# Second and last FFN of a two-layer decoder: third weight chunk without its displaced head, and no one-column product ahead of it

## The chip, the cores and the metric

The kernel runs on one core of one Trainium2 chip. The metric is the device time of one execution in microseconds (us); the median of three runs stands for a kernel.

## The reference

A causal decoder trunk of two layers on 256 tokens of width 1024, all in float32. Each layer adds half an FFN, a mixer and half an FFN again; every FFN is a SwiGLU of width 2816:

```python
def swiglu(x, w_gate, w_up, w_down):
    return (jax.nn.silu(x @ w_gate) * (x @ w_up)) @ w_down

for layer in range(DEPTH):                                   # 2
    h = h + 0.5 * swiglu(rms_norm(h, ffn1_norm[layer]), ...)
    h = h + (ab_mixer if layer == 0 else c_mixer)(rms_norm(h, mix_norm[layer]))
    h = h + 0.5 * swiglu(rms_norm(h, ffn2_norm[layer]), ...)
return rms_norm(h, final_norm)
```

So there are four FFNs. The second (phase 2 in the kernel) is the one behind the first layer's mixer, the last (phase 5) the one behind the second layer's; the third (phase 3) follows the second at once.

## The kernel before

**Products.** Each float32 operand is split into a high part, rounded to the type fp32r, and a low part, the remainder. One product of two matrices is three on TensorE (`mm3`, lines 389 to 391): high by high, low by high, high by low. Activations lie transposed in SBUF, `xTh` and `xTl`, eight tiles k of 128 rows by 256 tokens. In the gate and up parts of an FFN a weight tile of 128x128 is what TensorE holds (loaded by the record PEld) and 256 columns of `xTh` or `xTl` stream past it.

**The weight stream.** `weight_chunks` lists all weights as chunks of 2048 columns per partition, in the order of use; a gate or up chunk is 8 tiles k of 256 columns. `Stream` loads each by DMA from SP's queue into one of three `raw` tiles (line 202), then splits it into one of four pairs `whi`, `wlo`: high part by ScalarE (ACT, line 250), low part by VectorE (DVE, line 257). A chunk without a head is split in two pieces of 1024 columns. `st.take()` hands a chunk to TensorE, `st.free()` gives it back.

**The order in an FFN.** Chunk n alternates gate and up. For chunk n the loop in `ffn` takes a chunk and makes 48 products of 256 columns into one PSUM bank (`colwise`): 24 with the chunk's first 128 columns, then 24 with the other half; the first chunk alone goes by parts of k (`TURNS`), since its input is still being made. After chunk 2 (`late` is 3) two products form the sums for the norm (lines 482, 483), and SiLU and the products with up follow on DVE and ACT (`gated`). After 22 chunks come the down projections; the last FFN does these with products of 512 columns in `finish`.

**Addresses.** A chunk's columns begin 16 elements into their tile (`SHIFT`), and buffers, `xTh` and `xTl` are laid out so that in the gate, up and down products of 256 columns the next weight tile and the running stream stand 16 elements apart, modulo 64. A chunk with `reset=3` (`RESET`, given in `weight_chunks` for the chunk numbers in `again`) has the first 128 columns of its tiles k = 0, 1, 2 elsewhere:

```python
h = w // 2
far = nk * w - reset * h + RESHIFT // LINE * LINE + RESHIFT     # 2048 - 384 + 0 + 52
def part(t, k):
    if k >= reset:
        return t[:, at(k) : at(k) + w]
    return Halves(*(t[:, a : a + h] for a in (far + k * h, shift + k * h)))
```

1664 is a multiple of 64, so these three tiles stand 52 elements from the stream, modulo 64, where all others stand 16. They are used by the first nine products of the chunk (3 tiles by 3 products): this is the head. Such a chunk is split in three pieces, 384, 384 and 1280 columns. Heads stand in all four FFNs and in both mixers; in the first and third FFN many stand behind groups of other products that are woven in (`seven_products`).

**The product of one column.** In phases 2 and 5, behind the second chunk (n = 1), `ffn` multiplies a tile of ones by one column of ones into a bank that nobody reads (line 817). It is plain float32, and the records show it as two matmuls. The chunk behind it, n = 2, is the one with the head.

**What orders the engines.** A scheduling layer writes each engine's program from the code; instructions on one engine run in that order, and engines wait for each other by semaphores. In the last FFN DVE also transposes x (`turn_back`, line 713) and SP stores the result (`away`).

Of the kernel before, what the change touches and what calls it, by code (L numbers as in the profile page):

```python
# [54 lines left out]
def weight_chunks():  # L55

    chunks = []

    def add(m, r, n, c0, c1, shift=0, cuts=(), reset=0, summed=False, kind="N"):
        chunks.append((m[:-1], m[-1], r, n, c0, c1, shift, cuts, reset, summed, kind))  # L60

    def cols(m, c0, w, cuts=(), reset=0):
        n = CH // w
        for k in range(0, KD, n):
            add(m, k * 128, n, c0, c0 + w, SHIFT if w == 256 else 0, cuts, reset)

    def ffn(name, layer, last=False, again=(2, 3), phase=None):
        first = len(chunks)
        wd = (f"{name}_w_down", layer)
        lag = LAGS.get(phase, FT)  # L70
        woven = phase in LAGS

        def seven(pair):
            add(wd, pair * 256, 2, 0, 512, MSHIFT, kind="S")

        for c in range(0, FF, 256):
            if len(chunks) == 0:
                for k in (0, 4):
                    add((f"{name}_w_gate", f"{name}_w_up", layer), k * 128, 4, c, c + 256, SHIFT,
                        (1, 2, 3) if k else (0.5, 1, 1.5, 2, 3))  # L80
                continue
            for m in ("gate", "up"):
                n = len(chunks)
                cuts = (6,) if first == 0 and n in again else ()
                cols((f"{name}_w_{m}", layer), c, 256, cuts,
                     RESET if n - first in again or woven and m == "gate" and c // 256 > lag else 0)
            if c // 256 >= lag:
                seven(c // 256 - lag)
        if last:
            for i in range(FT // 2):  # L90
                add(wd, i * 256, 2, 0, D, kind=LAST[i])
            return
        rest = list(range(FT // 2 - lag, FT // 2)) if woven else []
        behind = woven
        if lag > 2 and woven:
            seven(rest.pop(0))
        for c in range(512 if woven else 0, D, 256):
            for k, n in DOWN:
                add(wd, k * 128, n, c, c + 256, SHIFT, reset=RESET if behind or woven and (c, k) == (768, 16) else 0)
                behind = bool(rest)  # L100
                if rest:
                    seven(rest.pop(0))

    def mix(m, order, summed=False):
        for k in order[:4:2]:
            add(m, k * 128, 2, 0, D, SHIFT)
        for c in (0, 512):
            add(m, order[4] * 128, 4, c, c + 512, SHIFT, summed=summed and c == 0)

    ffn("ffn1", 0, again=(2,), phase=0)  # L110
    wab = ("ab_w_in", 0)
    cols(wab, 0, 256)
    cols(wab, 512, 256, reset=RESET)
    cols(wab, 1024, 512)
    cols(wab, 2048, 512)
    for c, n in ((1536, RESET), (1792, 0), (256, RESET), (768, RESET)):
        cols(wab, c, 256, reset=n)
    mix(("ab_w_out", 0), MIX1)
    ffn("ffn2", 0, again=(2,), phase=2)
    ffn("ffn1", 1, again=(), phase=3)  # L120
    wc = ("c_w_in", 0)
    for c in range(4):
        cols(wc, c * 256, 256, reset=RESET if c % 2 else 0)
        cols(wc, 1024 + c * 256, 256, reset=0 if c else RESET)
        if c % 2 == 0:
            cols(wc, 2048 + c * 256, 512)
    mix(("c_w_out", 0), MIX2, True)
    ffn("ffn2", 1, True, again=(2,))
    return chunks


# [215 lines left out]
def trunk(ctx: ExitStack, tc: tile.TileContext, a, out):  # L347
    nc = tc.nc
# [10 lines left out]
    def bank():  # L359
        return ps.tile([128, 512], F32, name="bank")  # L360

    st = Stream(tc, (raw_pool, hi_pool, lo_pool), a["weights"])
    for ms, _, _, n, c0, c1, *how in weight_chunks():
        st.add(n, len(ms) * (c1 - c0), *how)
# [8 lines left out]
    ones = cp.tile([128, 128], F32, name="ones")  # L373
# [19 lines left out]
    def split(hi, lo, src):  # L393
        return nc.scalar.activation(hi, src, AF.Copy), nc.vector.tensor_sub(lo, src, hi.bitcast(F32))  # L394
# [131 lines left out]
    def colwise(p, w, groups=((0, range(KD)), (1, range(KD)))):  # L526

        n = 0
        for j, ks in groups:
            cs = slice(j * 128, (j + 1) * 128)  # L530
            for k in ks:
                mm3(p[:, j * S : (j + 1) * S], w[0][k][:, cs], w[1][k][:, cs], xT["h"][:, k], xT["l"][:, k],
                    n == 0, n == 2 * KD - 1)
                n += 1
# [154 lines left out]
    def ffn(phase):  # L689
        nonlocal nxt  # L690
        with tc.tile_pool(name="fp", bufs=1) as fp:
# [16 lines left out]
            def turn_back(t):  # L708

                with tc.issue_after(nxt.low.ins):  # L710
                    turned = xn.rearrange("p (j k r) -> p j k r", j=4, k=KD)
                    for k in range(KD):
                        nc.vector.transpose(turned[:, :, k],
                                            x1(k)[:, t * 128 : (t + 1) * 128].rearrange("p (j c) -> p j c", j=4))
                    nc.sync.dma_start(away[t], xn)
# [35 lines left out]
            def seven_products(c):  # L751

                if not sevens:
                    sevens.extend(bank() for _ in range(4))
                w = st.take()
                plain = [[h[:, 2 * c + k, t * 128 : (t + 1) * 128] for h in hT] for k, t in ((0, 0), (1, 0), (1, 1))]
                s3, s1, s2, s4 = ([h[:, i] for h in summed[c]] for i in range(4))
                a11, a12, a22 = plain
                for i, (at, (sh, sl), q) in enumerate(((0, a11, 0), (1, a12, 2), (2, s4, 1), (3, a22, 6), (4, s1, 3),
                                                       (5, s2, 5), (6, s3, 4))):  # L760
                    b = sevens[at // 2][:, at % 2 * S : (at % 2 + 1) * S]
                    mm3(b, sh, sl, w[0][q], w[1][q], c == 0 and at % 2 == 0, c == FT // 2 - 1 and at in (1, 3, 5, 6))
                st.free()
                summed.pop(c)
# [27 lines left out]
            def sums_at(n):  # L792

                if (phase, n) in AHEAD:
                    ahead.append(begin_sums(fp, AHEAD.index((phase, n))))
                if (phase, n - 1) in AHEAD:
                    ahead.append(ahead.pop()())
                if (phase, n - 2) in AHEAD:
                    ahead.pop()()
# [4 lines left out]
            for n in range(FT):  # L804
                k, m = n - n % 2, n % 2
                if phase == n == 0:
                    with tc.manual_schedule():
                        ready += begin(fp)
                elif phase or n > 1:
                    p = bank()  # L810
                    w = st.take()
                    colwise(p, w, *(() if n else (TURNS,)))
                    st.free()
                    ready.append(p)
                if phase in (2, 5) and n == 1:

                    nc.tensor.matmul(bank()[:, :1], ones, ones[:, :1], start=True, stop=True)
                sums_at(n)
                if n == late - 1:
                    if phase not in (2, 5):  # L820
                        split(*parts[:2], nxt.acc[:, 0])
                    nxt.everywhere(*parts)
                    if last:
                        half = nxt.column(norm["half"], parts[3][:, :128], "halfcol")
                if last and n in (6, 9):
                    turn_back(n // 9)
                    flat = X.rearrange("p i c -> p (i c)")
                    if n == 9:
                        st.spare.append(flat[:, :CH])
                if last and n == late:  # L830
                    hS = [fp.tile(size, F32R, name=m) for m in ("hSh", "hSl")]
                if n == late:
                    for i in range(0, n, 2):
                        gated(i, *ready[i : i + 2])
                elif n > late and m == 1:
                    gated(k, *ready[-2:])
                if m == 1 and k // 2 >= lag:
                    seven_products(k // 2 - lag)
# [546 lines left out]


    ffn(0)
    ab_mixer(1)
    ffn(2)
    ffn(3)  # L1390
    c_mixer(4)
    ffn(5)
# [19 lines left out]
def _layout(a):  # L1412

    def tiles(m):
        return m.reshape(-1, 128, m.shape[-1]).transpose(1, 0, 2)

    chunks = weight_chunks()
    weights = np.zeros((len(chunks), 128 * CH), np.float32)
    for j, (ms, layer, r, n, c0, c1, *how) in enumerate(chunks):
# [43 lines left out]
```

## Time and profile before

| | before |
|---|---|
| median of 3 runs | 920.46 us (920.32 to 920.67) |
| the profiled execution's own time | 919.95 us |
| its span | 918.2 us |
| TensorE (PE) busy | 910.9 us, 99%, 7533 matmuls |
| DVE busy, ACT busy | 774.4 us (84%), 562.4 us (61%) |
| chain that ended last | PE 99% |
| granted TensorE clock | 0.999 of full |
| the one-column products (line 817) | from 283.08 and from 748.44 us |

Times in the views are us from the span's start. A row of the timeline is start, length, engine, line, operation, output <- inputs, shape, and the count of merged records. A matmul's record lasts longer than the step to the next one, since matmuls overlap: a product of 256 columns has a record of 0.28 us and starts 0.11 us behind the one before. So PE is "busy" throughout, and what tells its speed is the step from start to start, or a count of products over a stretch. The clock does not appear in a row of the timeline; the view of stretches has it.

### The profile page before, as it was taken

The numbers are of one execution on the slowest core, as the hardware profiler recorded it, in microseconds if no ns is written. First come the engines' busy times: TensorE is split into PE (matmuls) and PEld (weight loads), VectorE is DVE, ScalarE is ACT, GpSimd is POOL, SyncE is SP. The second block draws the span as 40 slices with busy tenths as digits, with TensorE's granted clock in tenths as the row PEclk, the third lists the DMA queues.
The fourth block names the chain that finished last, engine by engine and source line by source line (L and its number), as shares of the span: only waits on it lengthen the run. The fifth ranks groups of instructions, "written<-read, shape, count | busy, mean of one in ns | idle before, by whom it ended". The sixth has DMA issues, their size and how long they took to land.

```text
span 918.2 us, 18470 instructions
## 1 busy us (share of the span) xinstructions
PE 910.9 (99%) x7533; PEld 892.0 (97%) x7533; DVE 774.4 (84%) x1269; ACT 562.4 (61%) x875; POOL 81.3 (9%) x117
## 2 busy tenths in 40 slices
PE   9999999999999999999999999999999999999997
PEld 9999999989999999999999999999999999999886
DVE  7999897997889777767799888878778799978897
ACT  7766555668667545444566555556777776555574
POOL 0000000034310000000000000001665100000001
PEclk9999999999999999999999999999999999999999
DMA  9646655664257779698746655466433566855691
GB/s 327 249 161 225 216 180 195 242 227 183 93 184 266 279 282 352 233 369 308 259 153 238 252 211 195 167 260 210 166 139 138 138 226 215 274 211 190 228 316 52
DMA packets 35428, 202.17 MB, mean 220 GB/s; under 512 B 4064, under 2 KB 6368, under 8 KB 14992
## 3 DMA queue, kind: packets, MB, share of 16 engines
q1 hardware_dynamic: 33840, 197.79, 60.1%
q0 software_dynamic: 496, 1.77, 0.9%
q10 hardware_dynamic: 1008, 1.44, 0.5%
q8 instruction: 59, 0.97, 0.4%
q14 instruction: 25, 0.20, 0.1%
HBM read 188.14 MB, written 12.85 MB: 219 GB/s over the span
## 4 chain that ended last, share of the span: by engine, by line
PE 99%; issue 0%; DVE 0%; POOLq 0%; POOL 0%; DVEq 0%
PE bank L389 31%; PE bank L390 31%; PE bank L391 31%; PE bank L1165 1%; PE bank L637 1%; PE bank L613 0%; PE bank L640 0%; PE bank L1127 0%; PE bank L1129 0%; PE bank L1128 0%; PE bank L923 0%; PE bank L919 0%; PE bank L920 0%; PE bank L1314 0%; PE bank L789 0%
## 5 line engine op out<-in xcount | busy, mean ns | idle before, releaser
L250 ACT ACTIVATE whi<-raw 128x1024 fp32r<-128x1024 f32 (+5 forms) x392 | 351.6, 942 | 219.1 <-PE bank L390 143.1
L257 DVE TENSOR_TENSOR wlo<-raw,whi 128x1024 fp32r<-128x1024 f32 (+5 forms) x392 | 414.4, 1084 | 37.1 <-ACT whi L250 36.2
L389 PE MATMUL bank<-xTh,whi 128*128 128x256 f32 x1600 | 442.9, 277 | 0.0
L390 PE MATMUL bank<-xTl,whi 128*128 128x256 f32 x1600 | 442.0, 276 | 0.0
L391 PE MATMUL bank<-xTh,wlo 128*128 128x256 f32 x1600 | 441.9, 276 | 0.0
L390 PEld LDWEIGHTS bank<-xTl,whi 128*128 128x128 f32 x1600 | 300.3, 188 | 0.3 <-DVE xTl L428 0.2
L389 PEld LDWEIGHTS bank<-xTh,whi 128*128 128x128 f32 x1600 | 300.3, 188 | 0.0
L391 PEld LDWEIGHTS bank<-xTh,wlo 128*128 128x128 f32 x1600 | 300.4, 188 | 0.0
L389 PE MATMUL bank<-hTh,whi 128*128 128x256 f32 x352 | 97.8, 278 | 0.0
L391 PE MATMUL bank<-hTh,wlo 128*128 128x256 f32 x352 | 97.4, 277 | 0.0
L390 PE MATMUL bank<-hTl,whi 128*128 128x256 f32 x352 | 97.4, 277 | 0.0
L389 PEld LDWEIGHTS bank<-hTh,whi 128*128 128x128 f32 x352 | 66.2, 188 | 0.0
L391 PEld LDWEIGHTS bank<-hTh,wlo 128*128 128x128 f32 x352 | 66.1, 188 | 0.0
L390 PEld LDWEIGHTS bank<-hTl,whi 128*128 128x128 f32 x352 | 66.1, 188 | 0.0
L724 DVE TENSOR_TENSOR hm<-gs,bank 128x512 f32<-128x512 f32 x44 | 29.9, 683 | 30.3 <-PE bank L391 30.1
L1060 POOL MEMSET k<- 64x256 f32 x12 | 3.3, 307 | 561.1 <-DVE x L439 560.9
L394 ACT ACTIVATE hSh<-gs 128x512 fp32r<-128x512 f32 (+1 forms) x31 | 18.6, 601 | 30.7 <-DVE gs L741 14.0
L389 PE MATMUL bank<-whi,hTh 128*128 128x256 f32 (+1 forms) x114 | 36.1, 316 | 0.0
L390 PE MATMUL bank<-wlo,hTh 128*128 128x256 f32 (+1 forms) x114 | 36.0, 316 | 0.0
L391 PE MATMUL bank<-whi,hTl 128*128 128x256 f32 (+1 forms) x114 | 36.0, 316 | 0.0
L389 PE MATMUL bank<-mixh,whi 128*128 128x256 f32 x128 | 35.7, 279 | 0.0
L1156 POOL TENSOR_SCALAR pr<-pr,rl 128x128 f32<-128x128 f32 (+1 forms) x36 | 33.2, 934 | 28.2 <-DVE rl L1152 19.2
(247 smaller groups left out, 1304.4 us busy)
## 6 DMA issues: line engine op xcount, KB each, us to landing
raw<-in_weights SPq DMA_DIRECT2D x131, 1024.0 KB, 5.0
raw<-in_weights SPq DMA_DIRECT2D x28, 512.0 KB, 3.6
blocks<-in_weights SPq DMA_DIRECT2D x9, 1024.0 KB, 8.2
blocks<-blocks SPq DMA_DIRECT2D x9, 1024.0 KB, 6.8
raw<-blocks SPq DMA_DIRECT2D x7, 1024.0 KB, 4.9
raw<-in_weights SPq DMA_DIRECT2D x8, 768.0 KB, 4.7
raw<-in_weights SPq DMA_DIRECT2D x7, 256.0 KB, 4.5
blocks<-block SPq DMA_DIRECT2D x5, 256.0 KB, 8.8
```

Of the source, the lines that this page charges most:

```text
L250: done = nc.scalar.activation(hi, r, AF.Copy)
L257: self.made[u] = done, nc.vector.tensor_sub(lo, r, hi.bitcast(F32))
L389: nc.tensor.matmul(p, sh, mh, start=start, stop=False)
L390: nc.tensor.matmul(p, sh, ml, start=False, stop=False)
L391: return nc.tensor.matmul(p, sl, mh, start=False, stop=stop)
L394: return nc.scalar.activation(hi, src, AF.Copy), nc.vector.tensor_sub(lo, src, hi.bitcast(F32))
L637: nc.tensor.matmul(o, w[0][i][:, cs], xT[m][:, k], start=k == 0 and m == "h" and j % 2 == 0, stop=False)
L724: nc.vector.tensor_mul(hm, g, both(pu))
L1060: nc.gpsimd.memset(pair[j][o, 1].bitcast(F32), 0.0)
L1156: share = engine.tensor_scalar(pr[:, cs], pr[:, cs], rl[:, b : b + 1], None, op0=ALU.mult)
L1165: nc.tensor.transpose(tp[:, i * 128 : (i + 1) * 128], pr[:, i * 128 : (i + 1) * 128], ident)
```

## The change

`again` is empty for the second and the last FFN, and the one-column product goes:

```diff
@@ weight_chunks @@
-    ffn("ffn2", 0, again=(2,), phase=2)
+    ffn("ffn2", 0, again=(), phase=2)
...
-    ffn("ffn2", 1, True, again=(2,))
+    ffn("ffn2", 1, True, again=())
@@ ffn @@
                     st.free()
                     ready.append(p)
-                if phase in (2, 5) and n == 1:
-
-                    nc.tensor.matmul(bank()[:, :1], ones, ones[:, :1], start=True, stop=True)
                 sums_at(n)
```

In the built program this removes one product in each of the two FFNs, moves the third chunk's head to the distance of 16 elements, and makes two pieces of its three splits.

TensorE at the end of the second FFN's second chunk, before (the numbers count buffers; `whi_3458` and `wlo_3459` are the second chunk, `whi_3560` and `wlo_3561` the third):

```order
L390 MATMUL bank_3659<-xTl_3407,whi_3458 128x256
L391 MATMUL bank_3659<-xTh_3406,wlo_3459 128x256
L817 MATMUL bank_3716<-ones_85 128x1
L389 MATMUL bank_3718<-xTh_3406,whi_3560 128x256
L390 MATMUL bank_3718<-xTl_3407,whi_3560 128x256
L391 MATMUL bank_3718<-xTh_3406,wlo_3561 128x256
```

and after:

```order
L390 MATMUL bank_3657<-xTl_3407,whi_3458 128x256
L391 MATMUL bank_3657<-xTh_3406,wlo_3459 128x256
L389 MATMUL bank_3714<-xTh_3406,whi_3560 128x256
L390 MATMUL bank_3714<-xTl_3407,whi_3560 128x256
L391 MATMUL bank_3714<-xTh_3406,wlo_3561 128x256
```

The third chunk's products follow the second's directly; the buffers are the same and only the columns of the nine products within them differ. Nothing else moves on TensorE, there or in the last FFN.

DVE in the last FFN around the splits of the third chunk, before (L257 is a low part, L459 and L462 are sums for the norm, L713 the transposes for `away`):

```order
L713 STREAM_TRANSPOSE xn<-x 128x4x32 x2
L462 TENSOR_TENSOR acc<-acc,sq 128x256
L257 TENSOR_TENSOR wlo<-raw,whi 128x384
L462 TENSOR_TENSOR acc<-acc,sq 128x256
L257 TENSOR_TENSOR wlo<-raw,whi 128x384
L713 STREAM_TRANSPOSE xn<-x 128x4x32 x2
L257 TENSOR_TENSOR wlo<-raw,whi 128x1280
L257 TENSOR_TENSOR wlo<-raw,whi 128x1024 x2
```

and after:

```order
L713 STREAM_TRANSPOSE xn<-x 128x4x32 x2
L462 TENSOR_TENSOR acc<-acc,sq 128x256
L713 STREAM_TRANSPOSE xn<-x 128x4x32
L462 TENSOR_TENSOR acc<-acc,sq 128x256
L257 TENSOR_TENSOR wlo<-raw,whi 128x1024 x4
```

The third chunk is the first two of the four low parts. One transpose stands ahead of them instead of two between them; the others come later. A few more of DVE's rows in the last FFN trade places in the next chunks, and on SP's queue the second store of `away` stands one weight load earlier:

```order
L715 DMA away_9401<-xn 128x1024
L202 DMA raw<-in_weights 128x2048 x8
```

before, with four weight loads between the two stores, and after with three:

```order
L715 DMA away_9395<-xn 128x1024
L202 DMA raw<-in_weights 128x2048 x9
```

On ACT the rows of line 250 change as the splits do, and none other.

## The prediction

> **What bounds the kernel now.** The page comes first: which engine ends the span, and whether it idles.
>
> ```profile
> span 918.2 us, 18470 instructions
> PE 910.9 (99%) x7533; PEld 892.0 (97%) x7533; DVE 774.4 (84%) x1269; ACT 562.4 (61%) x875; POOL 81.3 (9%) x117
> PE 99%; issue 0%; DVE 0%; POOLq 0%; POOL 0%; DVEq 0%
> ```
>
> TensorE is busy 99% and is 99% of the chain that ended last. So the time is a count of products times the step from one product's start to the next, and this case is about that step. The view of waits for PE has one row for the whole span:
>
> ```profile
> PE bank L613 <- PEq L1450: 0.8, 1, 0.8
> ```
>
> That is the kernel's start. What the two FFNs lose they lose in the step, not in a gap of idle time. The second view is the busy time in stretches: 272 to 283 are the second FFN's first two chunks, 284 to 485 the rest of it with the first chunks of the third FFN; 735 to 748 the end of the last mixer and the first two chunks of the last FFN, 750 to 858 the products of 256 columns behind them; 179.6 to 186.9 lies elsewhere, at the end of the first FFN and the start of the first mixer.
>
> ```profile
> 272.20:282.90 10.70, 10.70 (x97) 10.70 (x96) 10.12 (x18) 9.44 (x15) 0.00 (x0) 1.00 0.43 161
> 284.30:484.90 200.60, 200.60 (x1772) 200.60 (x1772) 153.93 (x193) 103.48 (x128) 0.00 (x0) 1.00 0.76 283
> 179.60:186.90 7.30, 7.30 (x64) 7.30 (x64) 7.30 (x12) 5.55 (x10) 0.96 (x4) 1.00 0.39 125
> 735.00:748.20 13.20, 13.20 (x118) 13.20 (x118) 12.65 (x27) 10.84 (x19) 0.00 (x0) 1.00 0.42 155
> 749.70:857.60 107.90, 107.90 (x954) 107.90 (x953) 91.72 (x153) 59.36 (x75) 0.56 (x1) 1.00 0.64 226
> ```
>
> The columns are the stretch, its length, PE busy with its count, PEld, DVE, ACT, POOL, then the granted clock. A record lasts 0.28 us and the next starts 0.11 later, so a count includes two products that had begun before the stretch. 200.60 us over 1770 products is 113.3 ns; 107.90 over 952 is 113.3; 13.20 over 116 is 113.8. But 7.30 over 62 is 117.7 ns. The clock is 1.00 in all of them, so the clock is not the difference. **There are two paces**, 113.3 and about 117.7 ns, for the same product. The second stretch at the slow pace, by its first and last row, and the rows in which one record's mean tells the paces apart (stretches 284.3 to 484.9 and 619.7 to 625.6):
>
> ```profile
> 619.59 0.28 PE L391 MATMUL bank<-hTh,wlo 128*128 128x256 f32 x1
> ...
> 625.60 0.28 PE L391 MATMUL bank<-hTh,wlo 128*128 128x256 f32 x1
> ```
> ```profile
> L389 PE MATMUL bank<-hTh,whi 128*128 128x256 f32 x176 | 48.6, 276 | 0.0
> ```
> ```profile
> L389 PE MATMUL bank<-hTh,whi 128*128 128x256 f32 x17 | 4.8, 281 | 0.0
> ```
>
> Fifty-one products in 6.01 us are 117.8 ns, and the records' mean is 281 ns against 276. So the slow pace costs 117.75 - 113.33 = 4.4 ns a product (113.33 is 200.60 over 1770), with no wait shown. It lasts until something disturbs it: the stretch that starts at 619.59 runs on through a change of chunk.
>
> **The change part by part.** The one-column product and the nine behind it, second FFN:
>
> ```profile
> 282.97 0.28 PE L391 MATMUL bank<-xTh,wlo 128*128 128x256 f32 x1
> 283.08 0.28 PE L817 MATMUL bank<-ones 128*128 128x1 f32 x2
> 283.22 0.36 PE L389 MATMUL bank<-xTh,whi 128*128 128x256 f32 x1
> 283.42 0.28 PE L390 MATMUL bank<-xTl,whi 128*128 128x256 f32 x1
> ...
> 284.13 0.28 PE L390 MATMUL bank<-xTl,whi 128*128 128x256 f32 x1
> 284.24 0.28 PE L391 MATMUL bank<-xTh,wlo 128*128 128x256 f32 x1
> ```
>
> and in the last FFN:
>
> ```profile
> 748.32 0.28 PE L391 MATMUL bank<-xTh,wlo 128*128 128x256 f32 x1
> 748.44 0.28 PE L817 MATMUL bank<-ones 128*128 128x1 f32 x2
> ...
> 749.60 0.28 PE L391 MATMUL bank<-xTh,wlo 128*128 128x256 f32 x1
> ```
>
> From 282.97 to 284.24 nine products of 256 columns start (the one at 282.97 and eight of the head) and the one-column product, which the records show as two. 1.27 us less 9 x 113.3 = 1.02 leaves 0.25 us. Of these, 283.08 to 283.22 is the product's own 0.14, the next step of 0.20 is 0.09 over the pace, and the rest of the head is 0.02 to 0.03. In the last FFN it is 1.28 less 1.02, 0.26 us. If the products of the third chunk then run at the pace, the gain is 0.25 + 0.26 = **0.51 us**; the trace puts nothing beside these products, since PE is the chain.
>
> The Trainium skill, "TensorE: Matmul & The Clock Gate", section "Wait — 56ns, not 53.3ns?", says that starts of matmuls never come closer than about 25 ns however few columns they have. By that alone two records in each FFN would be some 0.1 us in all, an estimate from that page; the rows give 0.14 each and 0.09 more behind it, and the rows are what I use. The same page, section "Step-by-step: what each phase is for", says that weights are loaded through a read port of their own and take nothing from the running matmul. By that the head at another distance would cost nothing; the trace disagrees, with steps of 115 to 120 ns in the head and two paces elsewhere.
>
> The splits of the third chunk change too. Each chunk is split into a high part (ACT, L250) and a low part (DVE, L257):
>
> ```profile
> L250 ACT ACTIVATE whi<-raw 128x1280 fp32r<-128x1280 f32 x28 | 35.3, 1261 | 0.0
> L250 ACT ACTIVATE whi<-raw 128x384 fp32r<-128x384 f32 x66 | 31.4, 515 | 19.3 <-PE bank L390 13.6 <-issue 2.5 <-ACT hTh L394 1.8
> L250 ACT ACTIVATE whi<-raw 128x1024 fp32r<-128x1024 f32 x249 | 252.8, 1052 | 149.0 <-PE bank L390 89.4 <-issue 30.6 <-DMA raw<-in_weights 9.6
> L257 DVE TENSOR_TENSOR wlo<-raw,whi 128x1024 fp32r<-128x1024 f32 x247 | 296.8, 1229 | 25.7 <-ACT whi L250 25.3
> ```
>
> On ACT 2 x 515 + 1261 = 2291 ns become 2 x 1052 = 2104. That is off the chain and worth nothing. What can hurt is that the first piece is larger: 1052 + 1229 ns until products can start. In the second FFN DVE ends these splits at 279.0, four us ahead of PE (first row below). In the last FFN they are closest:
>
> ```profile
> 276.53 2.48 DVE L257 TENSOR_TENSOR wlo<-raw,whi 128x384 fp32r<-128x384 f32 x3
> ```
> ```profile
> 744.38 3.98 ACT L250 ACTIVATE whi<-raw 128x384 fp32r<-128x384 f32 x5
> ```
> ```profile
> 743.72 0.30 DVE L713 STREAM_TRANSPOSE xn<-x 128x128 f32<-128x128 f32 x1
> ...
> 744.67 0.38 DVE L462 TENSOR_TENSOR acc<-acc,sq 128x256 f32<-128x256 f32 x1
> ...
> 745.44 0.42 DVE L462 TENSOR_TENSOR acc<-acc,sq 128x256 f32<-128x256 f32 x1
> ```
>
> ACT would have the first half at 744.38 + 1.05 = 745.4. By the new order DVE has the sum of 744.67, one transpose (0.30) and the sum that stood at 745.44 (0.42) in front of it, which end by 745.8, so the low half is there at about 747.0 and the second, 1.23 later, at 748.2. PE wants the first at 748.44 and the second twelve products later, at 749.8. The cover is some 1.5 us on both (748.44 less 747.0, 749.8 less 748.2). If it were gone, PE would wait a microsecond at most, once: bounds 0 to 1.0 us, and I take 0.
>
> One bank of PSUM less is taken in turn, and the second away transfer of the last FFN moves one weight load earlier on SP's queue; with no wait of PE on a bank or a load in this trace I cost both at nothing. If a moved load were late, the cover is the same 1.5 us.
>
> **What the head is there to hold off** is the term that decides the sign. Without it the second FFN runs on from 282.97 in the pace that it has. That is the fast one: from 273.68 to 282.97, 82 products in 9.29 us are 113.3 ns. In the last FFN the stretch from 735.00 is at 113.8 or less up to the one-column product. From then on all products keep one distance of addresses, and the 1770 behind the head show no later event that throws the pace. So by this trace nothing makes it slow: cost 0. Against that stands what came just before:
>
> ```profile
> 273.19 0.28 PE L389 MATMUL bank<-xTh,whi 128*128 128x256 f32 x1
> 273.31 0.30 PE L390 MATMUL bank<-xTl,whi 128*128 128x256 f32 x1
> 273.44 0.28 PE L391 MATMUL bank<-xTh,wlo 128*128 128x256 f32 x1
> ...
> 273.68 0.28 PE L390 MATMUL bank<-xTl,whi 128*128 128x256 f32 x1
> ```
>
> At 273.31 PE took 0.13 us for a step, for the low part of the input that DVE was only then finishing. After such a disturbance the pace is settled anew, and it can settle slow: the slow stretch from 619.59 on follows four transposes among the products (first row), and a head of nine that began at 178.60 ended in the slow pace of the stretch from 179.6 on:
>
> ```profile
> 618.91 0.60 PE L789 MATMUL bank<-ident,hm 128*128 128x128 f32 x4
> ```
> ```profile
> 178.37 0.28 PE L390 MATMUL bank<-hTl,whi 128*128 128x256 f32 x1
> 178.48 0.28 PE L391 MATMUL bank<-hTh,wlo 128*128 128x256 f32 x1
> 178.60 0.28 PE L389 MATMUL bank<-hTh,whi 128*128 128x256 f32 x1
> ```
>
> **The rivals.** (1) *The slow pace sets in and nothing ends it.* Place: second FFN, from 284.24, or last FFN, from 749.60. Price: 1770 x 4.4 = 7.8 us and 952 x 4.4 = 4.2 us. It decides where the pace at the end of the second chunk is the slow one. For it: the head is the only thing in either FFN that could set the pace; two stretches fell slow; the 0.13 us step depends on when DVE ends, so another execution may settle otherwise. Against it: both FFNs reach the head at the fast pace here, the four known times lie within 0.72 us, and the last FFN meets no disturbance after the mixer. (2) *The third chunk's weights come late:* 1.0 us, so 0.5 us slower in sum; against it the 1.5 us of cover. (3) *The change does nothing:* the third chunk could keep its split or PE its order. By the built program the product is gone and the splits are merged, so this needs the 0.51 us to be hidden by something that PE waits for at once; the view of waits shows none. (4) *A larger gain:* runs without the profiler may lose more in the step than the profiled one. For it, the median is 0.51 us above the profiled execution; against it, only the first two chunks could be slow today, at 96 x 4.4 = 0.4 us each, and the change would not mend them.
>
> **How the numbers follow.** The profiled execution took 919.95 us (918.2 of span and 1.75 around it), the runs 920.32 to 920.67 with a median of 920.46; the sum applies to either, and I state it on the median: 920.46 - 0.51 = 919.95. About 0.2%, 1.8 us, can be told from no change here, so this is "same". Chances: forecast 0.60. Rival 1 0.34: second FFN alone 0.13, 919.95 + 7.8 = 927.75; last FFN alone 0.09, 924.15; both 0.12, 931.95. Rival 2 0.02, 920.95; rival 3 0.02, 920.46; rival 4 0.02, below 918.6. Same is 0.60 + 0.02 + 0.02 = 0.64, slower 0.34, faster 0.02. The likeliest case's own range is 919.2 to 920.7, the spread of 0.72 among the known times on either side. The range for all cases goes up to the slow second FFN with half that spread, 928.2, and leaves out the double case and the larger gain, 0.14.
>
> **What would show it.** Right: no row of L817; steps of 0.11 through 282.97 and 748.44; group means of 276 ns for the products of 256 columns in both FFNs; the span 0.5 shorter. Rival 1: means of 281 ns there, with the granted clock still 1.00 and no wait of PE, and the slow pace ended by the third FFN's first head. Rival 2: a wait of PE for L257 near 748 or 750. The prediction is wrong if the pace behind the second chunk is not the pace within it.

## The result, and the profile after

The kernel with the change took 928.34 us in the median of 20 runs (919.24 to 929.34), the kernel before 920.68 (920.32 to 921.73, 20 runs). The ratio of the means is 1.0052 with an interval of 1.0032 to 1.0072: slower by half a per cent. But the median hides what happened. The 20 runs lie in two groups with nothing between them: 7 at 919.24 to 919.87, and 13 at 927.89 to 929.34. Seven executions were faster than any of before; the other thirteen lie 9 us above those seven and 8 us above the median of before (the groups' medians are 919.60 and 928.65 us). The kernel before has one group. The profiled execution of after belongs to the upper group, 928.97 us.

Its page:

```profile
span 927.3 us, 18458 instructions
PE 919.9 (99%) x7529; PEld 901.3 (97%) x7529; DVE 773.6 (83%) x1267; ACT 561.0 (60%) x873; POOL 82.1 (9%) x117
```

Four matmul records fewer than before, 7529 against 7533, and PE busy 9.0 us longer. The view of waits for PE still has the kernel's start alone:

```profile
PE bank L613 <- PEq L1447: 0.8, 1, 0.8
```

So no wait that this view shows has come in. The stretches (their columns are those of the prediction) say where the time is:

```profile
274.10:283.00 8.90, 8.90 (x78) 8.90 (x77) 8.32 (x13) 8.11 (x11) 0.00 (x0) 1.00 0.33 112
284.30:493.60 209.30, 209.30 (x1779) 209.30 (x1779) 155.30 (x194) 103.06 (x128) 0.00 (x0) 1.00 0.74 271
498.00:510.00 12.00, 12.00 (x104) 12.00 (x103) 11.86 (x19) 6.02 (x8) 0.00 (x0) 1.00 0.87 306
512.00:518.00 6.00, 6.00 (x55) 6.00 (x54) 5.03 (x9) 3.02 (x4) 0.00 (x0) 1.00 1.00 335
...
750.00:858.00 108.00, 108.00 (x955) 108.00 (x954) 94.40 (x161) 64.05 (x82) 0.56 (x1) 1.00 0.62 227
```

Two products less than each count began within its stretch. 209.30 over 1777 is 117.8 ns, the slow pace; 8.90 over 76 is 117.1, 12.00 over 102 is 117.6. From 512 on it is the fast one again, and the last FFN has it throughout: 108.00 over 953 is 113.3. The clock is 1.00 in all five. The means of one record in the second and in the fifth stretch say the same, 282 against 277 ns:

```profile
L389 PE MATMUL bank<-hTh,whi 128*128 128x256 f32 x176 | 49.6, 282 | 0.0
```
```profile
L391 PE MATMUL bank<-xTh,wlo 128*128 128x256 f32 x318 | 87.9, 277 | 0.0
```

Where it starts is in the timeline of PE, ten us ahead of the place that the change edits:

```profile
273.76 0.28 PE L391 MATMUL bank<-xTh,wlo 128*128 128x256 f32 x1
273.87 0.28 PE L389 MATMUL bank<-xTh,whi 128*128 128x256 f32 x1
273.98 0.29 PE L390 MATMUL bank<-xTl,whi 128*128 128x256 f32 x1
274.11 0.28 PE L391 MATMUL bank<-xTh,wlo 128*128 128x256 f32 x1
274.23 0.28 PE L389 MATMUL bank<-xTh,whi 128*128 128x256 f32 x1
274.34 0.28 PE L390 MATMUL bank<-xTl,whi 128*128 128x256 f32 x1
274.46 0.28 PE L391 MATMUL bank<-xTh,wlo 128*128 128x256 f32 x1
```

Steps of 0.11 up to 273.98, one of 0.13, and then 0.12 for good (0.35 for three steps, where the fast pace has 0.34). The product at 273.98 is the counterpart of that at 273.31 in before: the first that takes a low part which DVE has only just made. DVE's four low parts, before and after:

```profile
272.29 1.66 DVE L428 SCALAR_TENSOR_TENSOR xTl<-x,gT,xTh 128x256 fp32r<-128x256 f32 x4
```
```profile
272.96 1.66 DVE L428 SCALAR_TENSOR_TENSOR xTl<-x,gT,xTh 128x256 fp32r<-128x256 f32 x4
```

The second of the four, 0.48 us long, starts at 272.68 and at 273.35, and so ends at 273.16 and 273.83. PE's product starts 0.15 later in both, at 273.31 and 273.98. In the five other profiles that keep this order of the first chunk (the experiments below) it is 0.15 us too, though the low part ends anywhere from 273.04 to 274.07; so the product waits for it, though the view of waits has no row for so short a one. It is the same short wait, which makes one step 10 to 20 ns longer; before came out of it at the fast pace, and this execution of after at the slow one. The seam that the change made is clean, without a row of L817:

```profile
283.88 0.28 PE L390 MATMUL bank<-xTl,whi 128*128 128x256 f32 x1
284.00 0.28 PE L391 MATMUL bank<-xTh,wlo 128*128 128x256 f32 x1
284.12 0.28 PE L389 MATMUL bank<-xTh,whi 128*128 128x256 f32 x1
284.24 0.28 PE L390 MATMUL bank<-xTl,whi 128*128 128x256 f32 x1
```

The slow pace goes through it and ends in the third FFN, right behind the second of its heads, whose nine products start at 510.02 to 510.96:

```profile
510.96 0.28 PE L391 MATMUL bank<-xTh,wlo 128*128 128x256 f32 x1
511.07 0.29 PE L389 MATMUL bank<-xTh,whi 128*128 128x256 f32 x1
511.20 0.28 PE L390 MATMUL bank<-xTl,whi 128*128 128x256 f32 x1
511.32 0.28 PE L391 MATMUL bank<-xTh,wlo 128*128 128x256 f32 x1
511.43 0.28 PE L389 MATMUL bank<-xTh,whi 128*128 128x256 f32 x1
```

From 273.98 to 511.2 there are 237.2 us, at 117.8 ns some 2010 products, and 2010 x 4.4 ns are 8.9 us. With 0.7 us by which this execution came late to 272 and the gain of 0.5 us, that is the 9.1 us between the spans.

### The profile page after: what moved, and what is told of

Same layout as the page of the kernel before. It is cut to its first block, busy times and chain, and to the rows that moved or that the text cites. A ratio compares the mean times of both kernels' runs of the same rounds, so it can differ in the third digit from the quotient of the medians.

```text
span 927.3 us, 18458 instructions
## 1 busy us (share of the span) xinstructions
PE 919.9 (99%) x7529; PEld 901.3 (97%) x7529; DVE 773.6 (83%) x1267; ACT 561.0 (60%) x873; POOL 82.1 (9%) x117
## 4 chain that ended last, share of the span: by engine, by line
PE 94%; issue 3%; DMA 1%; POOL 0%; DVE 0%; ACT 0%; POOLq 0%; DVEq 0%
PE bank L390 30%; PE bank L389 30%; PE bank L391 30%; DMA x<-blocks 1%; PE bank L637 1%; PE bank L1162 1%; PE bank L640 0%; PE bank L613 0%; POOL xTl L906 0%; DVE wlo L257 0%; DMA xTl<-away 0%; PE bank L1124 0%; PE bank L1126 0%; PE bank L1125 0%; PE bank L1311 0%
## 5 line engine op out<-in xcount | busy, mean ns | idle before, releaser
L250 ACT ACTIVATE whi<-raw 128x1024 fp32r<-128x1024 f32 (+4 forms) x390 | 351.3, 945 | 236.5 <-PE bank L390 121.0
L257 DVE TENSOR_TENSOR wlo<-raw,whi 128x1024 fp32r<-128x1024 f32 (+5 forms) x390 | 414.1, 1090 | 43.2 <-ACT whi L250 42.3
L721 DVE TENSOR_TENSOR gs<-bank,row 128x512 f32<-128x512 f32 x44 | 29.9, 684 | 9.1 <-PE bank L391 9.0
L394 ACT ACTIVATE hSh<-gs 128x512 fp32r<-128x512 f32 (+1 forms) x31 | 18.6, 601 | 29.3 <-DVE gs L741 12.1
```

The lines of the kernel that those rows point to most:

```text
L250: done = nc.scalar.activation(hi, r, AF.Copy)
L257: self.made[u] = done, nc.vector.tensor_sub(lo, r, hi.bitcast(F32))
L721: nc.vector.tensor_mul(g, both(pg), twice(norm["row"]))
```

## The experiments

The theory from these rows: the short wait for the low part settles the pace anew in every execution; in before, the product with the head behind it brings either pace back to the fast one, so that nothing shows; the change takes that away. Its rivals: the changed columns or the seam themselves are slow, or something in the last FFN is. All kernels ran beside runs of before on the same chip, whose medians were 920.49 to 920.69. They ran on three chips: second_only, last_only and the two with pairs on one, head_only, product_only, late_plain and same_distance on another, the four from made_slow to slow_both on a third. "Low" counts the executions at 919 to 922 us, "high" those above.

| | median us | low | high | ratio to before, interval |
|---|---|---|---|---|
| second_only | 920.41 | 8 | 4, 928.80 to 930.20 | 1.0028, 1.0002 to 1.0055 |
| last_only | 920.30 | 11 | 0 | 0.9997, 0.9988 to 1.0005 |
| after_pairs | 919.94 | 11 | 0 | 0.9993, 0.9985 to 1.0002 |
| before_pairs | 920.37 | 11 | 0 | 0.9997, 0.9988 to 1.0006 |
| head_only | 932.96 | 0 | 4, 932.63 to 933.26 | 1.0135, 1.0122 to 1.0148 |
| product_only | 920.49 | 10 | 2, 928.74 and 929.77 | 1.0016, 0.9995 to 1.0037 |
| late_plain | 920.68 | 9 | 3, 925.21 to 925.57 | 1.0013, 1.0000 to 1.0026 |
| made_slow | 928.71 | 0 | 4, 928.32 to 929.14 | 1.0089, 1.0075 to 1.0103 |
| slow_product | 928.50 | 0 | 4, 928.39 to 928.71 | 1.0087, 1.0073 to 1.0101 |
| slow_head | 920.07 | 11 | 0 | 0.9996, 0.9987 to 1.0005 |
| slow_both | 920.27 | 11 | 0 | 0.9999, 0.9991 to 1.0008 |
| same_distance | 919.97 | 11 | 0 | 0.9992, 0.9983 to 1.0001 |

**Which half of the change.** second_only makes the change in the second FFN alone, last_only in the last alone:

```diff
@@ second_only, against before @@
-    ffn("ffn2", 0, again=(2,), phase=2)
+    ffn("ffn2", 0, again=(), phase=2)
-                if phase in (2, 5) and n == 1:
+                if phase == 5 and n == 1:
@@ last_only, against before @@
-    ffn("ffn2", 1, True, again=(2,))
+    ffn("ffn2", 1, True, again=())
-                if phase in (2, 5) and n == 1:
+                if phase == 2 and n == 1:
```

> Only the second FFN is changed; the last FFN keeps its one-column product and head. Theory (the pace of the second FFN is settled by the short wait of its first chunk, anew in each execution, and nothing resets it): executions fall in two groups, about 920.2 and about 929.2, the slow one with 281 ns records in the second FFN. Rival (the slow pace belongs to the last FFN or needs both changes): one group at 920.2.

> Only the last FFN is changed; the second keeps its one-column product and head. Theory: one group, 0.25 us under the kernel before, about 920.4 against 920.7, since the last FFN meets no wait before its third chunk; the stretch from 274 to 283 may be at either pace, worth at most 0.4 us. Rival (the last FFN can fall slow too): a second group about 4.2 us higher.

The high group comes with the second FFN and not with the last. The profiled execution of last_only shows the theory's other half, since the second FFN in it is that of before:

```profile
274.20:282.90 8.70, 8.70 (x76) 8.70 (x75) 8.12 (x13) 8.01 (x13) 0.00 (x0) 1.00 0.31 99
284.90:484.90 200.00, 200.00 (x1767) 200.00 (x1766) 152.47 (x193) 103.82 (x128) 0.00 (x0) 1.00 0.77 284
```

8.70 over 74 is 117.6 ns: this execution had come out of the wait at the slow pace. Behind the product and the head it runs 200.00 over 1765, 113.3. So executions with the old second FFN fall slow there too, and lose 76 x 4.4 ns, 0.3 us, which no time of a whole run tells: this execution's 920.97 us lies within the 919.95 to 921.25 of before.

**Whether it is the wait.** The second FFN's first chunk goes by parts of k, so that its first products find what DVE has made. after_pairs and before_pairs, on after and on before, order it by pairs of k, both halves of the chunk at each pair, so that each low part is wanted later:

```diff
@@ after_pairs against after, before_pairs against before @@
+    PAIRS = tuple((j, ks) for ks in (range(2), range(2, 4), range(4, 6), range(6, 8)) for j in range(2))
-                    colwise(p, w, *(() if n else (TURNS,)))
+                    colwise(p, w, *(() if n else (PAIRS if phase == 2 else TURNS,)))
```

> The changed kernel, with the second FFN's first chunk taken in pairs of k (0 and 1 for both halves, then 2 and 3, and so on) instead of four k first: the low part for k = 3 is then wanted at about 273.98 instead of 273.30, and it is there at 273.2. Theory: no wait, so no new settling; all executions in the fast group at 919.2 to 919.9, records of 276 ns throughout. Rival (the third chunk without its head makes the pace slow by itself): still two groups, 919.6 and 928.6.

> The kernel before with the same order by pairs in the second FFN's first chunk. Theory: as before or up to 0.4 us faster, 920.3 to 920.7, one group; against the changed kernel with pairs it shows the price of the two products and heads alone, 0.51 us. Rival (the order by pairs is itself worth or costs something): more than 0.5 us off 920.7.

The high group is gone: 0 of 11 where after had 13 of 20 and second_only, on the chip that after_pairs ran on, 4 of 12. The count alone would be weak, since late_plain below keeps the wait in the second FFN and has no such execution in 12. With it stand the rows: in the profiles of after, second_only and last_only the steps are 112 to 115 ns up to the product that waits, 123 to 129 at it, and 117 to 119 behind it. The stretches of after_pairs:

```profile
272.20:282.90 10.70, 10.70 (x97) 10.70 (x96) 10.12 (x17) 9.75 (x15) 0.00 (x0) 1.00 0.41 160
...
284.90:484.90 200.00, 200.00 (x1767) 200.00 (x1766) 153.37 (x193) 102.91 (x127) 0.00 (x0) 1.00 0.76 283
```

The first has no step over 0.12; the second, without head or product, is at 113.3 ns. And the medians of the two kernels differ by 0.43 us, which is the change's gain with the pace kept out of it; the prediction's sum was 0.51. The executions of the two overlap (919.73 to 920.49 and 919.98 to 920.95), so the size is rough. after_pairs has the lowest median of this study, 8.4 us under that of after. Against before it is 0.75 us lower, with an interval that still reaches 1.0002, so that much is not clear of noise.

**Which of the two parts did the work.** head_only is before without the two products of one column, product_only is before without the two heads:

```diff
@@ head_only, against before @@
-                if phase in (2, 5) and n == 1:
-
-                    nc.tensor.matmul(bank()[:, :1], ones, ones[:, :1], start=True, stop=True)
@@ product_only, against before @@
-    ffn("ffn2", 0, again=(2,), phase=2)
+    ffn("ffn2", 0, again=(), phase=2)
-    ffn("ffn2", 1, True, again=(2,))
+    ffn("ffn2", 1, True, again=())
```

> The kernel before without the two one-column products; both third chunks keep their head of nine. Theory with the head as the cure: one group about 0.4 us under the kernel before, 920.2, as the head alone ends a slow pace. Rival (the head moves the pace on from where it is, and needs a fixed place to start from, which the one-column product gives): slow executions remain, at 929 for the second FFN, or 924.6 for the last, where a head that starts at the fast pace can end in the slow one.

> The kernel before without the two heads; the one-column products stay. Theory (the head does the work): two groups, near 920.6 and 929.5, as in the changed kernel. Rival (any stop of the stream, the one-column product alone, settles the pace): one group, at 920.6 if it settles fast, and if it settles slow at 920.6 + 8.9 + 4.2 = 933.7 in every execution.

That the head cures a slow pace and the product is idle falls here. head_only is the slowest kernel of all, in 4 of 4. Its timeline at the head, whose nine products start at 283.52 to 284.45, and two of its stretches:

```profile
283.18 0.28 PE L389 MATMUL bank<-xTh,whi 128*128 128x256 f32 x1
283.29 0.28 PE L390 MATMUL bank<-xTl,whi 128*128 128x256 f32 x1
283.40 0.28 PE L391 MATMUL bank<-xTh,wlo 128*128 128x256 f32 x1
...
284.57 0.28 PE L389 MATMUL bank<-xTh,whi 128*128 128x256 f32 x1
284.69 0.28 PE L390 MATMUL bank<-xTl,whi 128*128 128x256 f32 x1
284.81 0.28 PE L391 MATMUL bank<-xTh,wlo 128*128 128x256 f32 x1
```
```profile
284.90:484.90 200.00, 200.00 (x1700) 200.00 (x1699) 147.27 (x181) 98.93 (x123) 0.00 (x0) 1.00 0.75 278
...
756.00:855.00 99.00, 99.00 (x844) 99.00 (x843) 82.73 (x143) 56.27 (x72) 0.56 (x1) 1.00 0.66 228
```

Steps of 0.11 ahead of the head, of 0.12 behind it, and 200.00 over 1698 is 117.8 ns; the last FFN, 99.00 over 842, 117.6. This head, met at the fast pace, ends in the slow one. (By the theory an execution that the wait had left slow would have come out of the second FFN's head fast; none of these four did.) The price fits: some 1920 products from 284.6 to 511 and 952 in the last FFN, at 4.4 ns, are 12.6 us; less 0.14 to 0.23 for each of the two products, 12.1 to 12.3; the time is 12.4 above before. product_only leaves 2 of 12 high, as if the product alone left the pace as it came. Its profile shows that of the fast pace, 113.3 ns ahead of the product and behind it; slow_product, below, shows it of the slow one.

**A wait in the last FFN.** In after no execution fell slow there. late_plain, on after, takes the last FFN's first chunk in the plain order of the others, so that PE reaches its low parts earlier than DVE makes them:

```diff
@@ late_plain, against after @@
-                    colwise(p, w, *(() if n else (TURNS,)))
+                    colwise(p, w, *(() if n or phase == 5 else (TURNS,)))
```

> The changed kernel with the last FFN's first chunk in plain order (all eight k for the first 128 columns, then the other half), so that it must wait for the low part of the input at k = 6, which is ready near 739.9 against some 739.4 wanted. Theory (a wait settles the pace, anywhere): the last FFN falls slow too, in some executions or in all, 4.2 us on top of either group of the second FFN: up to four groups, 920.2, 924.4, 929.2, 933.4. Rival (the last FFN cannot fall slow): the two groups of the changed kernel, moved by the 0.3 to 0.6 us of the wait alone.

The wait is there: the view of waits for weight loads (PEld), from 735 to 750, has a row that the same view of after lacks.

```profile
PEld bank L390 <- DVE xTl L428: 0.3, 1, 0.3
```

Three of 12 are 4.8 us above the other nine, by the medians of the two groups. The last FFN's two first chunks and the rest, 96 + 9 + 952 products at 4.4 ns, are 4.7, so these would be its slow pace; the profiled execution is one of the nine, so it is argued from the size, not seen. No execution of this kernel shows the second FFN's 9 us, though its second FFN is that of after: how often the wait ends badly differs from one set of runs to the next (13 of 20 in after, 4 of 12 in second_only, here 0 of 12), second_only and late_plain ran on different chips, and why it differs stays open.

**What moves a slow pace.** To have the slow pace each time, made_slow gives after_pairs a head at the second FFN's second chunk, where after_pairs shows the fast pace. The other three add what before had behind it, the product, the third chunk's head, or (slow_both) the two together:

```diff
@@ made_slow, against after_pairs @@
-    ffn("ffn2", 0, again=(), phase=2)
+    ffn("ffn2", 0, again=(1,), phase=2)
@@ slow_product, against made_slow @@
+                if phase == 2 and n == 1:
+                    nc.tensor.matmul(bank()[:, :1], ones, ones[:, :1], start=True, stop=True)
@@ slow_head, against made_slow @@
-    ffn("ffn2", 0, again=(1,), phase=2)
+    ffn("ffn2", 0, again=(1, 2), phase=2)
```

> The changed kernel with the order by pairs (which alone stayed fast, 919.94) and one head put at the second FFN's second chunk, that is, a head met at the fast pace. The theory that a head shifts the pace from where it stands, and from the fast pace into the slow one: every execution slow in the second FFN, 929 (919.9 + 9), at 281 ns records from about 278 to the third FFN's second head. Rival (a head leads to the fast pace from anywhere, and in the run without the one-column products something else was slow): one group at 919.9 to 920.0.

> The kernel that is made slow at the second chunk, with the one-column product behind that chunk and no further head. If a stop of the stream settles the pace anew: fast again from 284, 919.9 + 48 products at 4.4 ns + 0.2 = 920.3 in every execution. If the product alone does not: 929.2, or a mix of both groups, as the two of twelve executions with the product alone say.

> The kernel that is made slow at the second chunk, with a second head at the third chunk and no one-column product. If a head moves the slow pace on to the fast one, as the head at 625.71 did in the kernel before: 920.2 in every execution. If it leaves it slow, as the third FFN's first head did in the changed kernel: 929.

> The kernel that is made slow at the second chunk, with product and head at the third as in the kernel before. The pair as a reset: fast from 284 whatever came before, 919.9 + 0.2 + 0.25 = 920.4 in every execution, one group. Rival (the kernel before was only spared by chance): a group near 929 remains.

The stretches of made_slow, slow_product, slow_head and slow_both:

```profile
284.90:484.90 200.00, 200.00 (x1700) 200.00 (x1699) 146.51 (x181) 99.02 (x122) 0.00 (x0) 1.00 0.76 278
498.00:509.00 11.00, 11.00 (x96) 11.00 (x95) 9.79 (x15) 5.02 (x7) 0.00 (x0) 1.00 0.90 296
```
```profile
284.90:484.90 200.00, 200.00 (x1700) 200.00 (x1700) 146.54 (x180) 98.67 (x123) 0.00 (x0) 1.00 0.76 278
498.00:509.00 11.00, 11.00 (x100) 11.00 (x99) 10.58 (x17) 5.45 (x7) 0.00 (x0) 1.00 0.88 298
```
```profile
284.90:484.90 200.00, 200.00 (x1767) 200.00 (x1767) 153.33 (x193) 102.88 (x127) 0.00 (x0) 1.00 0.77 283
```
```profile
284.90:484.90 200.00, 200.00 (x1767) 200.00 (x1766) 152.97 (x193) 102.85 (x127) 0.00 (x0) 1.00 0.76 283
```

1700 is the slow pace, 1767 the fast. Ahead of the third chunk all four are slow: by the starts from 279.5 to 282.9 their steps are 117.8 ns. One head turns fast into slow (made_slow), a second one turns it back (slow_head). The product alone leaves the slow pace as it is (slow_product). The product with the head ends fast from the slow pace (slow_both), and from the fast one as well, as before_pairs and the trace of before show. So the product's part is that the head behind it ends fast whatever it met. Not every head shifts the pace. Those of the third FFN that stand behind woven products leave a fast pace fast: in before the first of them starts at 487.45, and by the starts from 489.0 to 500.7 the pace behind it is 113.3 ns. Met at the slow pace they differ: the first of them, at 496, ends the slow pace in slow_product (100 in 11 us) and not in made_slow (96); what decides there stays open.

**What in the head it is.** A head differs from a plain chunk in its distance of addresses, and in the split in three pieces. same_distance is made_slow with the same pieces, which for this one chunk begin 36 elements lower, so that the nine products stand 16 elements from the stream like all others (NEAR is that chunk's number):

```diff
@@ same_distance, against made_slow @@
-        far = nk * w - reset * h + RESHIFT // LINE * LINE + RESHIFT
+        place = SHIFT if j == NEAR else RESHIFT
+        far = nk * w - reset * h + place // LINE * LINE + place
```

> The kernel that is made slow at the second chunk, with the head's three pieces moved by 36 elements, so that its nine products stand 16 elements from the stream like all others; splits, pieces and order are the same, and nine weight addresses are all that differs. If the distance is what shifts the pace: fast in every execution, 919.9 to 920.0, against 928.7. If the split in three pieces or the place of the pieces does it: slow, 928.7.

```profile
284.90:484.90 200.00, 200.00 (x1768) 200.00 (x1767) 153.51 (x193) 103.62 (x128) 0.00 (x0) 1.00 0.76 283
```

The pace stays fast. The two kernels ran on different chips, so their ratios to before are compared, 1.0089 and 0.9992: nine addresses are worth 0.97%, 8.9 us. The split in three pieces and the order of the work, which are those of made_slow, leave the time at that of after_pairs (0.9993). One other place was tried, so whether it is the distance to the stream or the place of the nine tiles in itself is not shown.

## Why the prediction was wrong

- **What bounds the kernel** was right: PE's step, with two paces of 113.3 and 117.8 ns at the same clock and no wait shown.
- **The gain of 0.51 us** fits. With the wait out of the way it is 0.43 us (before_pairs less after_pairs, which overlap), and in the profile of after the seam has no step over the pace. The seven low executions of after lie 1.08 us under the median of before. Some 0.3 us of that can be the slow pace ahead of the head, which executions of before can have; what makes the rest is open.
- **Splits, banks and loads at nothing:** right. PE has no wait but the kernel's start, and the last FFN runs at 113.3 behind its third chunk.
- **The step that failed** is "Without it the second FFN runs on from 282.97 in the pace that it has. That is the fast one", with the cost of 0 that followed. That the pace runs on was right, and is just what made it costly. That it is the fast one was read from one execution, and the 13 of 20 show that the pace there is drawn anew each time, by the wait for the low part (after against after_pairs, and the rows in which the pace changes at the product that waits). Nothing behind it then ends the slow pace in that FFN: 8.9 us in 13 of 20 executions in place of the 0. The row for it stood in the prediction, as the 0.13 us step at 273.31, but only as a reason for a rival.
- **An argument that carried nothing** was the one against rival 1, that both FFNs reach the head at the fast pace and that the known times lie within 0.72 us. The times of before cannot tell the pace ahead of the head, since product and head cancel it: the profiled execution of last_only ran slow there and lies within the times of before.
- **Rival 1 in the second FFN** is what happened. Its price of 7.8 us was too low, since it counted from 284.24 to 484.9 where the slow pace ran from 273.98 to 511.2: 8.9 us. So the median, 928.34, lies just above the range, which ended at 928.2 (927.75 with half of 0.72 is 928.1). The end was put wrongly too: the third FFN's first head did not end it, the second did.
- **Rival 1 in the last FFN** did not happen in any run of after, which fits the reason that stood against it, no disturbance behind the mixer. With one put there (late_plain), 3 of 12 lost the size of it, without a profile that shows where.
- **The head as the one thing that sets the pace** was half of it. Alone, among plain products, it shifts the pace, either way; behind the one-column product it sets it.

## What to carry to other kernels

A profile is one execution: before you take out a step that seems to do nothing, ask what the runs would look like if it cancelled something that varies, and look for the wait, however short, that varies it. Where matmuls run back to back, read the step from start to start or the count over a stretch, since the busy share, the waits and the clock were alike at both paces; and read the runs as a list, since here the median of one kernel fell in one of two groups 9 us apart. Taking the wait away (after_pairs, 919.94 us) held the fast pace without a reset behind it, and was no slower than with it (before_pairs, 920.37).

## What the runs showed of the hardware

That TensorE has two lasting paces for the same product was in the trace of before. New is how it passes from one to the other: nine products at 52 elements from the stream instead of 16, modulo 64, shift it from fast to slow (made_slow) and from slow to fast (slow_head) where plain products stand ahead of them, and 1700 products at one distance keep what they were given. The Trainium skill, "TensorE: Matmul & The Clock Gate", section "Step-by-step: what each phase is for", says that weights are loaded through a read port of their own, so that loading them takes no read bandwidth of SBUF from the running matmul. A price of nothing for where the weights lie, which that suggests, is not what same_distance against made_slow shows: 8.9 us for nine addresses of weights and no other difference in the program. Whether the read ports are the reason, no run here shows.

In the seven profiled executions that had the short wait, its size goes with the outcome. By the starts in ns, the step of the product that waited was 18 to 19 ns over the pace, and the step ahead of it 4 to 5, in before, head_only, product_only and late_plain, which came out fast. It was 10 to 16 ns over, with at most 2 ahead, in after, second_only and last_only, which came out slow. That a longer wait saves and a shorter one harms was not tried, so it is a pattern of seven and no cause. What the two paces are within the engine also stays open.
